# Layer norm behind the experts: offsets and one over the deviation brought by the transposing products

## The chip, the core and the metric

The kernel runs on one core of a Trainium2 chip. Its engines are TensorE (PE, with its weight load PEld), VectorE (DVE), ScalarE (ACT), GpSimd (POOL) and SyncE (SP); each takes its own instructions strictly in order and waits on semaphores for the others. The metric is the device time of one execution in microseconds (us), lower is better.

## What is computed

Two blocks of two layers each on 256 tokens of width 1024. The change sits at the end of both layers of the first block, in the layer norm behind the mixture of experts:

```python
for l in range(DEPTH):                    # two layers
    mix = hybrid_mixer(h, ...)            # attention
    x = layer_norm(ALPHA * x + mix, ln1_g[l], ln1_b[l])
    ffn = grouped_moe(x, ...)             # 16 experts, 2 of them for each token
    x = layer_norm(ALPHA * x + ffn, ln2_g[l], ln2_b[l])   # here
```

with y = (x - mean) * rsqrt(var + eps) * g + b along the 1024 columns of a token. Behind the first layer comes the second layer's mixer, behind the second layer the first mixer of the second block (a gated linear recurrence).

## The kernel before

The 256 tokens stand as two blocks of 128 rows (b = 0, 1), the 1024 columns as two halves (q = 0, 1). Every matrix product of a weight with the tokens wants the tokens transposed, and split into a high part (`xh`, rounded by ACT) and a low part (`xl`, the rest, subtracted by DVE); products are then high by high, low by high and high by low. Weights are split in the same way.

In `moe` the experts go in eight pairs. `down` (products `pdn`) gives a pair's rows, split into `oh` and `ol`; `spread` adds them to the token rows in four PSUM banks `py[b][q]`, eight products a pair. While the last pair is under way, `pre()` prepares the next part's first weights: `ready` rounds them on ACT (line 215) and subtracts on DVE, or on POOL for the units named by `pool` (line 217). This is `mixer_first` (products `pk` follow, in `mixer`) behind the first layer and `hgrn_first` (products `pv`, in `hgrn`) behind the second.

Then 16 filler products (`warm`, line 224) are queued on PE, and `layer_norm` runs. For each block: two statistics and their merge on DVE, the square root on ACT, and for each half two DVE steps (line 393): (y - mean) * g, and times one over the deviation plus b. The result `xn` is turned by four PE transposes (line 228) into a bank `pt`, which ACT reads as `xh` (line 363) and DVE subtracts to `xl` (line 364). DVE's steps follow each other in the order written, through `issue_after`; where no such tie is given, a scheduler puts the instructions of each engine in order when the program is built. The fields `s.after` tie the first five weight splits of the next part (line 166, 167) behind the norm.

A `pb` bank is one of four PSUM banks, a `pa` bank one of four others.

Of the kernel before, what the change touches and what calls it, by code (L numbers as in the profile page):

```python
# [10 lines left out]
F32 = mybir.dt.float32  # L11
F32R = mybir.dt.float32r
# [3 lines left out]
AF = mybir.ActivationFunctionType  # L16
ALU = mybir.AluOpType
# [3 lines left out]
T = 256  # L21
# [9 lines left out]
WM = 16  # L31
# [47 lines left out]
class Halves:  # L79


    def __init__(s, tiles):
        s.t = tiles
# [13 lines left out]
class Net:  # L97
# [7 lines left out]
    def __init__(s, ctx, tc, A, dump=None):  # L105
        s.ctx, s.tc, s.nc, s.A, s.dump = ctx, tc, tc.nc, A, dump or {}
        e = ctx.enter_context
        s.cp = e(tc.tile_pool(name="cp", bufs=1))
        s.ring = e(tc.tile_pool(name="ring", bufs=s.RING))
        s.weave, s.steps = None, 0  # L110
        s.after = []
        s.st = e(tc.tile_pool(name="st", bufs=1))
        s.dr = e(tc.tile_pool(name="dr", bufs=1, space=bass.MemoryType.DRAM))
        s.ps = e(tc.tile_pool(name="ps", bufs=4, space=bass.MemoryType.PSUM))
        s.consts()
# [44 lines left out]
    def split(s, h, l, src, g=None, pool=False):  # L160
        nc = s.nc
        with ExitStack() as es:
            for ins in s.after[:1] and s.after.pop(0):
                es.enter_context(s.tc.issue_after(ins))
            if g is None:
                nc.scalar.activation(h, src, AF.Copy)  # L166
                i = (nc.gpsimd if pool else nc.vector).tensor_tensor(l, src, h.bitcast(F32), op=ALU.subtract)  # L167
                s.low = i.ins
            else:
                nc.scalar.activation(h, src, AF.Copy, scale=g)  # L170
                nc.vector.scalar_tensor_tensor(l, src, g, h.bitcast(F32), op0=ALU.mult, op1=ALU.subtract)
# [33 lines left out]
    def ready(s, pieces, n=512, pool=()):  # L205

        s.units = []
        for k0 in range(0, 8, 2):
            if k0 % 4 == 0:
                H, L = (s.raw().bitcast(F32R)[:, :4 * n].rearrange("p (k n) -> p k n", k=4) for _ in range(2))  # L210
                s.units.append((k0, H, L))
            k = slice(k0 % 4, k0 % 4 + 2)
            for c0, src in pieces(k0):
                c = slice(c0, c0 + src.shape[2])
                s.nc.scalar.activation(H[:, k, c], src, AF.Copy)
                e = s.nc.gpsimd if k0 // 2 in pool else s.nc.vector
                e.tensor_tensor(L[:, k, c], src, H[:, k, c].bitcast(F32), op=ALU.subtract)

    def warm(s, n):

# [158 lines left out]
    def layer_norm(s, y, gb, out=None, added=False):  # L379


        nc, v = s.nc, s.nc.vector
        sl = [slice(q * 512, (q + 1) * 512) for q in range(2)]
        st = [s.st.tile([128, 2, 6], F32, tag="bst", name="bst", bufs=2) for _ in range(2)]
        mv = [s.st.tile([128, 4], F32, tag="mv", name="mv", bufs=2) for _ in range(2)]
        x = lambda b, q: s.xn[:, b, sl[q]]
        prev, low, act = [], {}, []

        def dve(f, *a, **k):
            with ExitStack() as es:  # L390
                for i in prev[-1:]:
                    es.enter_context(s.tc.issue_after(i))
                prev.append(f(*a, **k).ins)  # L393

        def moments(b, q):
            if not added:
                dve(v.scalar_tensor_tensor, x(b, q), x(b, q), ALPHA, y[b][q], op0=ALU.mult, op1=ALU.add)
            dve(v.bn_stats, st[b][:, q], y[b][q] if added else x(b, q))
            if q:
                dve(v.bn_aggr, mv[b][:, 0:2], st[b])  # L400
                act.append(nc.scalar.activation(mv[b][:, 2:3], mv[b][:, 1:2], AF.Sqrt, bias=s.eps[:, 0:1]).ins)

        def affine(b, q):
            dve(v.scalar_tensor_tensor, x(b, q), y[b][q] if added else x(b, q), mv[b][:, 0:1], gb[:, 0, sl[q]],
                op0=ALU.subtract, op1=ALU.mult)
            if not q:
                dve(v.reciprocal, mv[b][:, 3:4], mv[b][:, 2:3])
            dve(v.scalar_tensor_tensor, x(b, q), x(b, q), mv[b][:, 3:4], gb[:, 1, sl[q]], op0=ALU.mult, op1=ALU.add)
            if out is not None:
                nc.sync.dma_start(out[b * 128:(b + 1) * 128, sl[q]], x(b, q))  # L410
            else:
                a, low[b, q] = s.xT_high(s.xn[:, b], b, q)
                act.append(a.ins)

        def lows(*bq):
            for i in bq if out is None else ():
                dve(low[i])
        with s.tc.high_priority():
            for q in range(2):
                moments(0, q)  # L420
            for q in range(2):
                affine(0, q)
            for q in range(2):
                moments(1, q)
            lows((0, 0), (0, 1))
            for q in range(2):
                affine(1, q)
            lows((1, 0), (1, 1))
        s.after = [(act[-1], prev[-1])] * 5


    def rms(s, p, n, pool):
# [618 lines left out]
    def moe(s, li, y, pre):  # L1051
        nc, A = s.nc, s.A
        v = nc.vector
        with ExitStack() as es:
            mp = es.enter_context(s.pool("mo"))
# [14 lines left out]
            py = [[], []]  # L1070
# [15 lines left out]
            xTe, PT = {}, {}  # L1086

            def sources():

                for p in range(9):  # L1090
                    for n, w, k, m in (("g", A["w_gate"], 8, p), ("u", A["w_up"], 8, p), ("d", A["w_down"], 4, p - 1)):
                        if 0 <= m < 8:
                            o = "e (k p) f -> p e k f" if n == "d" else "e (p k) f -> p e k f"
                            wv = w[li, 2 * m:2 * m + 2].rearrange(o, p=128)
                            for k0 in range(0, k, k // 4):
                                yield wv[:, :, k0:k0 + k // 4]
            src = list(sources())
            place = list(islice(chain(s.FILL, cycle([c for c in s.FILL if c not in "mpx"])), len(src)))
            n0, loaded, todo = len(s.FILL), {}, iter(range(len(src)))
            m = s.FILL.index("m")  # L1100
# [3 lines left out]
            def load(i):  # L1104
                if i < len(src) and i not in loaded:
                    loaded[i] = s.chunks(src[i], place[i])
# [7 lines left out]
            def onehot(g):  # L1114

                es_ = slice(4 * g, 4 * g + 4)
                P = mp.tile([128, 2, 4, 64], F32R, tag="P", name="P")
                for b in range(2):
                    i = v.tensor_tensor(P[:, b], s.iota[:, None, :].to_broadcast([128, 4, 64]),
                                        rs[:, b, es_, None].to_broadcast([128, 4, 64]), op=ALU.is_equal).ins  # L1120
                return P, i
# [61 lines left out]
            def turn(ac):  # L1183
                pt = s.pb("pat")
                for c in range(4):
                    s.tr(pt[:, c * 128:(c + 1) * 128], ac[:, c * 128:(c + 1) * 128])
                v.tensor_copy(aT, pt.rearrange("p (c e s) -> p c e s", c=4, e=2))
# [22 lines left out]
            with s.tc.manual_schedule(engines={mybir.EngineType.PE}):  # L1210
                P, i = onehot(0)
                with s.tc.issue_after(i):
                    for c in (0, 4):
                        low_rows(v, 1, slice(c, c + 4))
                i = slots(0, P)
                for p in range(8):
                    ac = gate_up(p, None if p else lambda: gates(0, P))
                    if not p:
                        with s.tc.issue_after(i):
                            residual()  # L1220

                        for j in range(n0):
                            load(j)
                    if p:
                        os_[p - 1] = down()
                    turn(ac)
                    if p >= 2:
                        spread(p - 2, *os_.pop(p - 2))
                    if p % 2 and p < 7:
                        slots(p // 2 + 1, onehot(p // 2 + 1)[0])  # L1230
                    if p == 2:
                        s.overflow(li, ga, ov, rs, cnt, xnh, xnl, py)
                spread(6, *os_[6])
                o = down()
                gb = s.load_gb(s.places, A["ln2_g"][li], A["ln2_b"][li], "raw5")
                pre()
                s.xh, s.xl = s.new_xT()
                spread(7, *o)
            s.warm(WM)
            s.layer_norm(py, gb, added=True)  # L1240


    def hgrn_first(s):
# [355 lines left out]
```

## Time and profile before

| what | value |
|---|---|
| median of 3 runs | 1365.07 us |
| lowest and highest run | 1357.44 and 1366.09 us |
| profiled execution | 1362.14 us, of it 1360.4 us span on the engines |
| PE busy in the span | 1303.4 us (96%) |
| DVE, ACT, POOL busy | 769.6, 587.5, 79.0 us |
| first layer norm behind the experts | about 361 to 377 us in the span |
| second one | about 720 to 740 us in the span |

The profile is of one execution; its places are given in microseconds from the span's start. PE is the engine that is busy nearly all the time, so what counts is where PE waits, and how much work it is given.

### The profile page before, as it was taken

How to read it: one execution, taken by the hardware profiler on the slowest of the kernel's cores; microseconds unless marked ns; L12 is line 12 of the kernel's file. 1: busy time of each engine (PE TensorE's matmuls, PEld its weight loads, DVE VectorE, ACT ScalarE, POOL GpSimd, SP SyncE). 2: the span in 40 equal slices, each digit the busy share in tenths (PEclk: the TensorE clock that was granted, in tenths of full speed). 3: DMA queues.
4: the chain of work that ended last, by engine and by line, in shares of the span. 5: the costliest groups of instructions: out<-in, count | busy, mean ns of one | idle time of the engine just before them, and what ended most of it. 6: DMA issues, size and time to landing. Idle time of an engine off the chain costs nothing.

```text
span 1360.4 us, 20419 instructions
## 1 busy us (share of the span) xinstructions
PE 1303.4 (96%) x7933; PEld 950.2 (70%) x7933; DVE 769.6 (57%) x1611; ACT 587.5 (43%) x1107; POOL 79.0 (6%) x94
## 2 busy tenths in 40 slices
PE   7899999999989999999998999999999999999997
PEld 6787543443488663443445988889998787899986
DVE  4775520110468562111116678879885677888855
ACT  5585410110266841110104424456665376566642
POOL 3000100000200010000002143000000000000000
PEclk8899999999999999999999999999999999999999
DMA  9585799999984478999999730565553465565500
GB/s 300 194 310 182 259 410 407 409 409 408 351 302 155 157 267 334 409 408 409 409 408 330 249 124 1 186 216 191 187 212 125 133 210 184 181 224 186 206 12 31
DMA packets 153639, 343.03 MB, mean 252 GB/s; under 512 B 13377, under 2 KB 84999, under 8 KB 153536
## 3 DMA queue, kind: packets, MB, share of 16 engines
q1 hardware_dynamic: 149408, 330.14, 66.4%
q0 software_dynamic: 3808, 11.24, 2.4%
q8 instruction: 66, 1.08, 0.3%
q10 hardware_dynamic: 320, 0.26, 0.1%
q14 instruction: 37, 0.30, 0.1%
HBM read 340.53 MB, written 1.07 MB: 251 GB/s over the span
## 4 chain that ended last, share of the span: by engine, by line
PE 51%; DVE 3%; ACT 1%; issue 1%; DMA 1%; POOL 0%; ACTq 0%; DVEq 0%
PE pb L174 19%; PE y L174 12%; PE pv L174 3%; PE pdn L174 3%; PE pgg L174 3%; PE pgu L174 3%; PE pl L174 2%; PE ptk L174 2%; DVE xn L393 1%; PE py L174 1%; PE pkv L174 1%; PE po L174 1%; PE pt L228 1%; DVE wl L167 1%; DMA raw<-in_hgrn_w_in 1%
## 5 line engine op out<-in xcount | busy, mean ns | idle before, releaser
L167 DVE TENSOR_TENSOR wl<-raw,wh 128x1024 fp32r<-128x1024 f32 (+1 forms) x208 | 248.3, 1200 | 86.2 <-ACT wh L166 84.3
L166 ACT ACTIVATE wh<-raw 128x1024 fp32r<-128x1024 f32 (+1 forms) x208 | 213.7, 1035 | 70.2 <-PE y L174 62.1
L174 PE MATMUL pb<-xh,wl 128*128 128x256 f32 (+1 forms) x944 | 132.5, 281 | 1.6 <-DVE wl L167 1.6
L174 PE MATMUL pb<-xh,wh 128*128 128x256 f32 (+1 forms) x944 | 133.5, 281 | 0.5 <-ACT wh L166 0.5
L174 PE MATMUL pb<-xl,wh 128*128 128x256 f32 (+1 forms) x944 | 132.4, 280 | 0.0
L1180 DVE SCALAR_TENSOR_TENSOR misc<-misc,gs,pgu 128x512 f32<-128x512 f32 x16 | 12.0, 748 | 208.6 <-PE pgu L174 145.3
L174 PEld LDWEIGHTS pb<-xh,wh 128*128 128x128 f32 (+1 forms) x944 | 120.3, 187 | 2.1 <-ACT wh L166 0.7
L174 PEld LDWEIGHTS pb<-xh,wl 128*128 128x128 f32 (+1 forms) x944 | 119.9, 187 | 2.2 <-DVE wl L167 2.0
L174 PEld LDWEIGHTS pb<-xl,wh 128*128 128x128 f32 (+1 forms) x944 | 119.9, 187 | 0.1
L174 PE MATMUL pgg<-raw,xTe 128*64 128x512 f32 x480 | 108.1, 602 | 5.2 <-PEq L1011 5.2
L174 PE MATMUL pgu<-raw,xTe 128*64 128x512 f32 x512 | 112.7, 592 | 0.0
L174 PE MATMUL pdn<-raw,misc 128*64 128x512 f32 x496 | 109.3, 592 | 0.0
L166 ACT ACTIVATE xh<-pdn 128x512 fp32r<-128x512 f32 x32 | 19.1, 597 | 195.6 <-PE pdn L174 195.6
L174 PEld LDWEIGHTS pgu<-raw,xTe 128*64 128x64 f32 x512 | 37.2, 137 | 71.3 <-issue 65.7
L174 PEld LDWEIGHTS pdn<-raw,misc 128*64 128x64 f32 x496 | 36.1, 137 | 69.7 <-issue 68.0
L174 PEld LDWEIGHTS pgg<-raw,xTe 128*64 128x64 f32 x480 | 34.3, 138 | 69.4 <-issue 60.7
L167 DVE TENSOR_TENSOR xl<-pdn,xh 128x512 fp32r<-128x512 f32 x32 | 22.0, 687 | 100.4 <-ACT xh L166 94.4
L1179 ACT ACTIVATE misc<-pgg 128x512 f32<-128x512 f32 x16 | 9.6, 597 | 138.8 <-PE pgg L174 138.8
L174 PE MATMUL y<-wl,gh 128*128 128x512 f32 x176 | 68.7, 390 | 0.0
L174 PE MATMUL y<-wh,gl 128*128 128x512 f32 x176 | 68.6, 390 | 0.0
L174 PE MATMUL y<-wh,gh 128*128 128x512 f32 x176 | 68.2, 389 | 0.0
L174 PE MATMUL y<-wl,xh 128*128 128x512 f32 x128 | 51.6, 404 | 0.0
(381 smaller groups left out, 2238.6 us busy)
## 6 DMA issues: line engine op xcount, KB each, us to landing
raw<-in_w_up SPq DMA_DIRECT2D x128, 512.0 KB, 10.2
raw<-in_w_down SPq DMA_DIRECT2D x124, 512.0 KB, 10.2
raw<-in_w_gate SPq DMA_DIRECT2D x120, 512.0 KB, 10.2
raw<-in_ffn_w_in SPq DMA_DIRECT2D x44, 1024.0 KB, 5.6
raw<-in_ffn_w_out SPq DMA_DIRECT2D x22, 1024.0 KB, 4.9
raw<-in_hgrn_w_in SPq DMA_DIRECT2D x16, 1024.0 KB, 9.4
raw<-in_w_o SPq DMA_DIRECT2D x8, 1024.0 KB, 11.4
raw<-in_w_in SPq DMA_DIRECT2D x6, 1024.0 KB, 7.5
```

What stands on the lines that cost most here:

```text
L166: nc.scalar.activation(h, src, AF.Copy)
L167: i = (nc.gpsimd if pool else nc.vector).tensor_tensor(l, src, h.bitcast(F32), op=ALU.subtract)
L174: s.last = s.nc.tensor.matmul(out, lhsT, rhs, start=start, stop=stop, skip_group_check=True).ins
L228: return s.nc.tensor.transpose(out, in_, s.ident[:k, :k])
L393: prev.append(f(*a, **k).ins)
L1179: nc.scalar.activation(sg, ps[0], AF.Silu)
L1180: v.scalar_tensor_tensor(ac, sg, gs[:, p:p + 1], ps[1], op0=ALU.mult, op1=ALU.mult)
```

## The change

A new function `sum_norm` takes the place of `layer_norm` in `moe`. DVE makes only (y - mean) * g. ACT writes `dg`, the identity with row t scaled by one over the deviation of token t. The turned tile is now a sum of two products in PSUM: the offsets (b's columns by the identity, `offsets`) and xn by `dg` (`turned`). `xn` itself gets its factor and offset in four DVE steps at the end. Further, `s.behind` ties the rounding of the next part's first weights behind the last pair's own rounding, and the DVE subtractions of those weights are held (`s.held`) and issued inside `sum_norm`, half of them between the blocks' statistics and half behind the first block's low parts.

```diff
@@ in split
-                nc.scalar.activation(h, src, AF.Copy)
+                s.high = nc.scalar.activation(h, src, AF.Copy).ins
@@ in ready
-                s.nc.scalar.activation(H[:, k, c], src, AF.Copy)
-                e = s.nc.gpsimd if k0 // 2 in pool else s.nc.vector
-                e.tensor_tensor(L[:, k, c], src, H[:, k, c].bitcast(F32), op=ALU.subtract)
+                with ExitStack() as es:
+                    if s.behind:
+                        es.enter_context(s.tc.issue_after(s.behind))
+                    s.nc.scalar.activation(H[:, k, c], src, AF.Copy)
+                low = (src, H[:, k, c].bitcast(F32), L[:, k, c])
+                if s.behind and k0 // 2 not in pool:
+                    s.held.append(low)
+                else:
+                    e = s.nc.gpsimd if k0 // 2 in pool else s.nc.vector
+                    e.tensor_tensor(low[2], low[0], low[1], op=ALU.subtract)
@@ new
+    def sum_norm(s, y, gb, dg):
...
+        def seq(f, *a, **k):
+            e = id(f.__self__)
+            with ExitStack() as es:
+                if e in last:
+                    es.enter_context(s.tc.issue_after(last[e]))
+                last[e] = f(*a, **k).ins
+        act = nc.scalar.activation
+
+        def moments(b):
+            for q in range(2):
+                seq(v.bn_stats, st[b][:, q], y[b][q])
+            seq(v.bn_aggr, mv[b][:, 0:2], st[b])
+            seq(act, mv[b][:, 2:3], mv[b][:, 1:2], AF.Sqrt, bias=s.eps[:, 0:1])
+
+        def centred(b, q):
+            seq(v.scalar_tensor_tensor, x(b, q), y[b][q], mv[b][:, 0:1], gb[:, 0, sl[q]], op0=ALU.subtract,
+                op1=ALU.mult)
+            if not q:
+                seq(v.reciprocal, mv[b][:, 3:4], mv[b][:, 2:3])
+                seq(act, dg[:, b], s.ident, AF.Copy, scale=mv[b][:, 3:4])
+
+        def offsets(q):
+            p = s.pb("pt")
+
+            for j in range(4):
+                c = 4 * q + j
+                s.mm(p[:, j * 128:(j + 1) * 128], gb[:, 1, c * 128:(c + 1) * 128], s.ident, not j, False)
+            return p
+
+        def turned(b, q, p):
+            for j in range(4):
+                c = slice((4 * q + j) * 128, (4 * q + j + 1) * 128)
+                s.mm(p[:, j * 128:(j + 1) * 128], s.xn[:, b, c], dg[:, b], False, True)
+            pv = p.rearrange("p (a t) -> p a t", a=4)
+            h, l = (m.t[q][:, :, b * 128:(b + 1) * 128] for m in (s.xh, s.xl))
+            seq(act, h, pv, AF.Copy)
+            low[b, q] = lambda: seq(v.tensor_tensor, l, pv, h.bitcast(F32), op=ALU.subtract)
...
+        n = len(s.held) // 2
+        with s.tc.high_priority():
+            ps = [offsets(q) for q in range(2)]
+            moments(0)
+        s.warm(WM)
+        with s.tc.high_priority():
+            for q in range(2):
+                centred(0, q)
+                turned(0, q, ps[q])
+            held(n)
+            moments(1)
+            for q in range(2):
+                low[0, q]()
+            held(n)
+            for q in range(2):
+                centred(1, q)
+                turned(1, q, offsets(q))
+            for q in range(2):
+                low[1, q]()
+        s.after = [(last[id(nc.scalar)], last[id(v)])] * 5
+        for b in range(2):
+            for q in range(2):
+                seq(v.scalar_tensor_tensor, x(b, q), x(b, q), mv[b][:, 3:4], gb[:, 1, sl[q]], op0=ALU.mult, op1=ALU.add)
@@ in moe
+                s.behind = s.high
                 pre()
+                s.behind = None
...
-            s.warm(WM)
-            s.layer_norm(py, gb, added=True)
+            dg = mp.tile([128, 2, T], F32R, tag="PT", name="dg", bufs=2).bitcast(F32)[:, :, :128]
+            s.sum_norm(py, gb, dg)
```

The change alters the order that the scheduler builds. The rows below are instructions as they stand in an engine's queue, with the line of the code, the operation, what it writes and reads, and its size; "x16" is so many in a row.

PE, at the end of the first layer's experts, before: the last pair's `down`, then its `spread` into the four banks.

```order
L174 MATMUL pdn<-raw,misc 64x512 x16
L174 MATMUL py<-xh,PT 128x512
L174 MATMUL py<-xl,PT 128x512
L174 MATMUL py<-xh,PT 128x512
L174 MATMUL py<-xl,PT 128x512
```

The same place now; `pt<-c,gb` is four products of offsets for a half (c holds the identity), `warm` is a filler.

```order
L175 MATMUL pdn<-raw,misc 64x512 x3
L175 MATMUL pt<-c,gb 128x128 x8
L175 MATMUL pdn<-raw,misc 64x512 x13
L175 MATMUL py<-xh,PT 128x512
L175 MATMUL py<-xl,PT 128x512
L175 MATMUL py<-xh,PT 128x512
L232 LDWEIGHTS negI
L232 MATMUL warm<-mgtb,negI 128x512
L232 LDWEIGHTS negI
L232 MATMUL warm<-mgtb,negI 128x512
L175 MATMUL pt<-c,gb 128x128 x4
L175 MATMUL py<-xl,PT 128x512
```

Eight offset products moved into the `down` products, and two fillers and four offset products ahead of the second half's low product. The second layer's end reads alike. Behind `spread` stand 13 fillers (14 in the second layer), then eight products `pt<-dg,xn`.

ACT, in the second layer's mixer behind the norm, before: the turned halves of block 1, the query and key norm's sums (`rmsj`, `rms`, `rmsn`: three steps for each block of `pk`) and the splits of the next weights (`wh`).

```order
L363 ACTIVATE xh<-pt 128x4x128 x2
L436 ACTIVATE rmsj,rms<-pk 128x256
L437 ACTIVATE rms<-rms,eps 128x1
L680 ACTIVATE rmsn<-pk,rms 128x256
L166 ACTIVATE wh<-raw 128x1024 x2
L166 ACTIVATE wh<-raw 128x8x64
L166 ACTIVATE wh<-raw 128x8x32
L166 ACTIVATE wh<-raw 128x768
L436 ACTIVATE rmsj,rms<-pk 128x256
```

The same place now.

```order
L455 ACTIVATE xh<-pt 128x4x128 x2
L521 ACTIVATE rmsj,rms<-pk 128x256
L522 ACTIVATE rms<-rms,eps 128x1
L765 ACTIVATE rmsn<-pk,rms 128x256
L521 ACTIVATE rmsj,rms<-pk 128x256
L522 ACTIVATE rms<-rms,eps 128x1
L765 ACTIVATE rmsn<-pk,rms 128x256
L167 ACTIVATE wh<-raw 128x1024 x2
```

The three steps of block 1 moved ahead of all the splits; PE's products `pb` behind `pk` need the first `wh`.

ACT, behind the second layer's norm, before: `V` is the copy of a finished block of `pv`, `lb` a small table for which another function table is loaded.

```order
L363 ACTIVATE xh<-pt 128x4x128
L1365 ACT_TABLE_LOAD
L1365 ACTIVATE lb<-lb 128x16
L166 ACTIVATE wh<-raw 128x1024
L1357 ACTIVATE V<-pv 128x512
L166 ACTIVATE wh<-raw 128x1024 x3
```

The same place now.

```order
L1445 ACTIVATE V<-pv 128x512
L1453 ACT_TABLE_LOAD
L1453 ACTIVATE lb<-lb 128x16
L1445 ACTIVATE V<-pv 128x512
L167 ACTIVATE wh<-raw 128x1024 x4
```

The copy of block 1 moved ahead of the first split, which the next `pv` products need.

## Rows read from the trace of the kernel before

**Rows 1.** Stretches: us, busy us (count) of PE, PEld, DVE, ACT, POOL, clock, DMA, GB/s

```profile
350.00:361.50 11.50, 11.50 (x55) 5.55 (x53) 2.09 (x4) 1.41 (x4) 0.00 (x0) 1.00 0.89 280
...
720.70:729.80 9.10, 6.77 (x31) 3.21 (x29) 8.82 (x11) 5.68 (x8) 4.73 (x2) 1.00 1.07 355
```

**Rows 2.** Timeline of the first norm: start, us, engine, line, operation [idle before <- released by]

```profile
354.46 7.09 PE L174 MATMUL pdn<-raw,misc 128*64 128x512 f32 x32
...
360.76 0.60 ACT L166 ACTIVATE xh<-pdn 128x512 fp32r<-128x512 f32 x1 [9.91 <-PE pdn L174]
...
364.02 0.50 PE L174 MATMUL py<-xl,PT 128*128 128x512 f32 x1 [1.10 <-DVE xl L167]
...
364.55 0.70 DVE L393 BATCH_NORM_STATS2 bst<-py 128x6 f32<-128x512 f32 x1 [0.59 <-PE py L174]
...
365.28 2.98 PE L224 MATMUL warm<-mgtb,negI 128*128 128x512 bf16 x13
...
368.10 0.60 PE L228 MATMUL pt<-c,xn 128*128 128x128 f32 x4
...
369.44 0.45 PE L174 MATMUL pk<-raw,xh 128*128 128x392 f32 x1
```

**Rows 3.** The single products of offsets' kind: timeline of PE at 398 us

```profile
398.21 5.40 PE L174 MATMUL px<-ikT,iqT 128*128 128x128 f32 x32
```

**Rows 4.** Timeline of the second norm

```profile
719.96 0.60 ACT L166 ACTIVATE xh<-pdn 128x512 fp32r<-128x512 f32 x1 [9.91 <-PE pdn L174]
...
722.17 0.50 PE L174 MATMUL py<-xl,PT 128*128 128x512 f32 x1
...
723.45 3.41 PE L224 MATMUL warm<-mgtb,negI 128*128 128x512 bf16 x15
...
725.07 5.49 POOL L217 TENSOR_TENSOR raw<-raw 128x1024 fp32r<-128x1024 f32 x2 [27.99 <-ACT raw L215]
...
725.68 2.65 DVE L393 SCALAR_TENSOR_TENSOR xn<-xn,mv,gb 128x512 f32<-128x512 f32 x1
...
729.79 0.50 PE L174 MATMUL pv<-raw,xh 128*128 128x512 f32 x1 [0.53 <-ACT xh L363]
```

**Rows 5.** Line 393's steps, by form: count, min/median/max ns, first and last start

```profile
L393 DVE SCALAR_TENSOR_TENSOR xn<-xn,mv,gb x40: 741/752/2651, 366.7 to 1356.5; 128x512 f32<-128x512 f32 x40
```

**Rows 6.** Timeline behind the first norm, in the second layer's mixer

```profile
376.87 0.38 ACT L436 ACTIVATE rmsj<-pk 128x256 f32<-128x256 f32 x1
...
378.28 3.56 ACT L166 ACTIVATE wh<-raw 128x1024 fp32r<-128x1024 f32 x5
378.32 1.59 PE L174 MATMUL pk<-raw,xh 128*128 128x392 f32 x8
...
380.46 1.46 PE L174 MATMUL pb<-xh,wh 128*128 128x256 f32 x11
...
382.64 1.21 PE L174 MATMUL pb<-xh,wl 128*128 128x256 f32 x8 [0.71 <-DVE wl L167]
```

**Rows 7.** Timeline behind the second norm

```profile
744.16 1.09 PE L174 MATMUL pv<-wh,xh 128*128 128x512 f32 x4
744.36 0.60 ACT L1357 ACTIVATE V<-pv 128x512 f32<-128x512 f32 x1 [1.95 <-PE pv L174]
744.85 2.94 ACT L166 ACTIVATE wh<-raw 128x1024 fp32r<-128x1024 f32 x3
...
747.22 0.73 PE L174 MATMUL pv<-wl,xh 128*128 128x512 f32 x2 [0.29 <-DVE wl L167]
```

**Rows 8.** The chain that ended last, behind the second norm: start, us, what

```profile
747.22 8.90 PE pv L174 x37
```

**Rows 9.** Timeline of PE after a wait in the experts, first and second layer

```profile
224.66 7.09 PE L174 MATMUL pgg<-raw,xTe 128*64 128x512 f32 x32 [2.78 <-PEq L1011]
...
582.17 8.76 PE L174 MATMUL pgg<-raw,xTe 128*64 128x512 f32 x32 [2.44 <-PEq L1011]
```

**Rows 10.** The stretch of the second of these waits, columns as in rows 1

```profile
580.00:584.00 4.00, 1.82 (x6) 0.69 (x8) 0.00 (x0) 0.00 (x0) 0.00 (x0) 0.77 1.02 402
```

More of the change, by code (lines that the diff above doesn't have):

```diff
@@ L111, in __init__ @@
         s.after = []
+        s.behind, s.held = None, []
         s.st = e(tc.tile_pool(name="st", bufs=1))
@@ L429, in layer_norm, with held @@
         s.after = [(act[-1], prev[-1])] * 5
+    def sum_norm(s, y, gb, dg):
+        nc, v = s.nc, s.nc.vector
+        sl = [slice(q * 512, (q + 1) * 512) for q in range(2)]
+        st = [s.st.tile([128, 2, 6], F32, tag="bst", name="bst", bufs=2) for _ in range(2)]
+        mv = [s.st.tile([128, 4], F32, tag="mv", name="mv", bufs=2) for _ in range(2)]
+        x = lambda b, q: s.xn[:, b, sl[q]]
+        last, low = {}, {}
+        def seq(f, *a, **k):
[30 more added lines that the diff above has]
+            low[b, q] = lambda: seq(v.tensor_tensor, l, pv, h.bitcast(F32), op=ALU.subtract)
+        def held(n):
+            for _ in range(n):
+                src, h, l = s.held.pop(0)
+                seq(v.tensor_tensor, l, src, h, op=ALU.subtract)
+        n = len(s.held) // 2
[21 more added lines that the diff above has]
+                seq(v.scalar_tensor_tensor, x(b, q), x(b, q), mv[b][:, 3:4], gb[:, 1, sl[q]], op0=ALU.mult, op1=ALU.add)
```

## The prediction

> **What bounds the kernel now.** I read the page first: PE is busy for 96% of the span, and the chain that ended last is mostly PE. So a change counts by the waits that it takes from PE, and by the work that it adds there. Then the stretches around the two norms [rows 1]. In the last `down` and what stands ahead of it PE has no gap at all: 11.50 us busy in 11.50. In the second norm it is busy for 6.77 of 9.10, and 3.41 of that is filler [rows 4]; about 5.7 us there are not work. Last the timelines, where the reader is to follow one thread: ACT rounds the last pair's rows, PE spreads them, DVE takes statistics, filler runs, PE turns the tile, ACT copies it, PE begins `pk` or `pv`. In the first norm that is 360.76, 364.02, 364.55, 365.28, 368.10 and 369.44 [rows 2].
>
> **The change, part by part.** The order of each queue is fixed when the program is built, so I follow the new order with the old durations.
>
> *Offsets in the `down` products.* A single product in full precision shows on PE as two records. The 32 records from 398.21 are eight products of 128 and eight of 256 columns, 48 units of 128 in 5.40 us: 0.11 a record, 0.225 a product of 128 [rows 3]. Eight offset products cost 1.8, and they stand where PE has no gap [rows 1], so all of it is on the path, once in each norm. The gap that might hide them would be a wait for weights there, and there is none in 354.46 to 361.5 [rows 2].
>
> *Last pair first.* In the first norm the second half's low product came 3.26 after the first rounding (360.76 to 364.02) [rows 2], since a weight's rounding and subtraction stood between. In the second it came 2.21 after (719.96 to 722.17) [rows 4]: the pair's parts stood first there already, and the new order moves nothing. Gain 1.05 in the first norm, 0 in the second.
>
> *Two fillers and four offsets ahead of that low product.* The four cost 0.9; a filler is 0.23 (2.98 for 13) [rows 2], and most of the two lies in PE's wait for DVE. I take 1.05, between 0.9 and 1.36. The last `py` product is later by 1.8 - 1.05 + 1.05 = 1.8 in the first norm, by 1.8 + 1.05 = 2.85 in the second.
>
> *Filler.* 13 of them now stand ahead of the first turning product. In the first norm they begin at 365.28 + 1.8 = 367.1 and end at 370.1. DVE's thread to the old transposes took 3.55 (364.55 to 368.10), and one step of 0.75 [rows 5] has left it, so its data is there some 0.5 or more before; the filler, which was cover, decides. Eight products (1.8) and one filler follow, so `pk` begins at 372.1 against 369.44: +2.65. In the second norm filler begins at 723.45 + 2.85 = 726.3, 14 take 3.2, then one offset, eight products and three offsets, 2.7: `pv` begins at 732.2 against 729.79, +2.4.
>
> The old second norm had a loss that goes: DVE's second step took 2.65 us [rows 4] where its median is 0.75 [rows 5], beside POOL's subtractions from 725.07 on. That step leaves the thread, which is why the second norm isn't worse by its 2.85; the new filler takes the rest. The held subtraction of DVE now stands beside POOL's second one. It may be stretched by nothing or by those 1.9; it delays block 1's statistics and so its `dg`, for which PE then waits. I take 1.0, the middle, in the second norm, and 0 in the first, where POOL's tiles are half as wide or less.
>
> The Trainium skill (SBUF — State Buffer, Who interferes with whom) says that a DVE instruction with both inputs in SBUF and a GpSimd instruction that reads SBUF share a port pair, and that the later one waits for all of the other. The row of 2.65 agrees. By the rule alone the held subtraction would wait as that step did, and the sum would be 0.9 more; without it, 1.0 less.
>
> *Turning block 1.* A `pk` product takes 0.18 (eight from 378.32 and four more until 380.46) [rows 6], 48 of them 8.55. Four offsets (0.9) and eight turning products (1.8) now lie among them: 372.1 + 11.25 = 383.35 against 380.46, +2.9. In the second norm a `pv` product takes 0.24 (8.90 for 37) [rows 8], 48 of them 11.55, with 1.8 of turning and the wait of 1.0: 746.55 against 744.16 [rows 7], +2.4.
>
> *ACT's order behind.* PE's next products `pb` need the first split `wh`. Before, ACT had begun it at 378.28, while PE was still at `pk` [rows 6]. Now the sums of block 1 stand ahead of it, and they need the end of `pk`. From a block's sums to the first split is 1.41 (376.87 to 378.28) [rows 6], the split itself 0.98 (2.94 for three) [rows 7], and a little to PE: 2.5 in which PE has nothing. `pb` begins 2.9 + 2.5 = 5.4 late. Of the old wait of 0.71 for the low split [rows 6] about 0.45 goes, since that split has time now: +4.95. The four deferred steps on `xn` stand ahead of block 0's small steps on DVE, 3 us long; they are over before `pk` ends and cost nothing by themselves. Behind the second norm block 1's `V` now stands ahead of the first split: it begins 0.2 after the last `pv` product and takes 0.5 (744.36 to 744.85) [rows 7], then 0.98 and 0.1: 1.8. With 0.3 of an old wait gone [rows 7], 2.4 + 1.8 - 0.3 = +3.9.
>
> Sum: 4.95 + 3.9 = 8.9 us. Behind both places the order is as before, and PE is nearly full there, so I let nothing be won back. Against the profiled execution's 1362.14 that is 1371.0. This execution lies 2.9 below the median of the runs shown (1365.07), which would give 1374.0; the runs spread from 1357.44 to 1366.09. I forecast 1372. From both sides: without ACT's waits and without `dg`'s 3.6 is left; with the stretches in full 10.
>
> **Rivals.** *The shorter thread decides (faster).* If PE's added products fall into its waits and filler, what is left is the gain: 1.05 of last pair first, 0.75 of the step that left the thread in each norm, and 1.9 of POOL's stretch: 4.45, so 1357.7. For it speaks that 5.7 us of the second norm are no work [rows 1, 4]. It decides as soon as the offsets in `down` find a gap and ACT reaches its splits before PE wants them. Against it: 11.50 of 11.50 [rows 1], and two queues whose order is plain.
>
> *The clock falls (slower by more).* The new waits of PE are 2.5 and 1.8. In the experts a wait of 2.78 left the next run of products at 7.09, a wait of 2.44 made the same run 8.76 [rows 9], and there the granted clock reads 0.77 [rows 10], so the clock went to the lower of its levels, 1.2 GHz, for a part of it. One such fall costs 1.7, one at each place 3.4: 1374 to 1376, on the median's side 1377.
>
> *It doesn't do what it says.* Last pair first does nothing in the second norm; that is in the sum already. Were it void in the first too, 1 more: 1373.
>
> **How the numbers follow.** The forecast with its small variants gets 0.62, 1366 to 1376. The clock gets 0.2, since one of two such waits fell. The shorter thread gets 0.18; its 1357.7 lies outside the range but part of its spread inside. A measurement of this kernel can tell about 1% from no change, here 13.65 us, above 1378.7 or below 1351.4. The forecast and the faster rival lie within that, and only the clock with underrated waits goes beyond: faster 0.02, within 0.88, slower 0.10. Range 1361 to 1380.
>
> **What the changed profile would show.** In the last `down`: eight products `pt<-c,gb` as one run of about 1.8 with no idle before it; idle there would favour the faster rival. In the second norm no step on `xn` from `py` above 0.8. Turning products that begin as the filler ends, ACT's copy long idle before: right; filler already over, and PE idle for `dg`: my thread of DVE is too short. A wait of PE for `wh` (ACT) of about 2.5 ahead of the first `pb` behind `pk`, and of about 1.8 ahead of `pv<-wh`: right; under 0.5: wrong by 4. A granted clock under 0.9 within a few us behind either: the second rival.
>
> What would make all of it wrong: a gain or loss far from the two norms, where the order is the same and I counted nothing, or a run of PE there that takes up the delay because its weights, not its inputs, come last.

## The result, and the profile after

The changed kernel takes 1377.42 us (median of 7 runs, 1371.15 to 1378.66), the kernel before in the same session 1362.44 (7 runs, 1357.44 to 1366.09). The ratio is 1.0101, 95% interval 1.0076 to 1.0125. The profiled execution of after took 1378.62, its span is 1376.6 against 1360.4.

The timeline of PE in the first norm, kernel after (start, us, engine, line, operation, idle before and who ended it):

```profile
356.51 1.93 PE L175 MATMUL pdn<-raw,misc 128*64 128x512 f32 x6
358.38 2.05 PE L175 MATMUL pt<-c,gb 128*128 128x128 f32 x16
360.36 6.22 PE L175 MATMUL pdn<-raw,misc 128*64 128x512 f32 x26
366.51 0.50 PE L175 MATMUL py<-xh,PT 128*128 128x512 f32 x1
...
370.22 2.98 PE L232 MATMUL warm<-mgtb,negI 128*128 128x512 bf16 x13
373.04 1.95 PE L175 MATMUL pt<-dg,xn 128*128 128x128 f32 x16
...
374.85 0.53 PE L175 MATMUL pk<-raw,xh 128*128 128x392 f32 x1
...
379.38 2.05 PE L175 MATMUL pt<-dg,xn 128*128 128x128 f32 x16 [0.29 <-ACT dg L455]
...
386.25 0.88 PE L175 MATMUL pk<-raw,xl 128*128 128x392 f32 x4
390.32 1.22 PE L175 MATMUL pb<-xh,wh 128*128 128x256 f32 x8 [3.19 <-ACT wh L167]
```

The first `py` product of the kernel before, on the same timeline:

```profile
361.48 0.49 PE L174 MATMUL py<-xh,PT 128*128 128x512 f32 x1
```

The reader is to see four things against it and [rows 2, 6]. From the first `down` product to the first `py` product it is 366.51 - 356.51 = 10.00, before 361.48 - 354.46 = 7.02. The turning products begin as the filler ends, with no idle time. Block 1's turning products wait 0.29 for `dg`. And ahead of `pb` PE has nothing for 3.19, where before it went straight on.

DVE, ACT and POOL (GpSimd) in the first norm and at that wait, kernel after, timelines of the three engines:

```profile
371.19 0.73 DVE L455 SCALAR_TENSOR_TENSOR xn<-py,mv,gb 128x512 f32<-128x512 f32 x1
371.84 2.76 DVE L455 TENSOR_TENSOR raw<-raw 128x512 fp32r<-128x512 f32 x2
...
377.12 1.03 DVE L455 TENSOR_TENSOR raw<-raw 128x512 fp32r<-128x512 f32 x2
...
382.70 2.73 DVE L455 SCALAR_TENSOR_TENSOR xn<-xn,mv,gb 128x512 f32<-128x512 f32 x4
...
387.17 0.17 DVE L683 TENSOR_SCALAR iw<-pk 128x8 f32<-128x8 f32 x1 [0.18 <-PE pk L175]
...
387.56 0.17 DVE L535 TENSOR_TENSOR ropet<-pk,c 128x16 f32<-128x16 f32 x1
```

```profile
371.31 0.40 ACT L455 ACTIVATE dg<-c,mv 128x128 f32<-128x128 f32 x1
...
387.82 0.38 ACT L521 ACTIVATE rmsj<-pk 128x256 f32<-128x256 f32 x1 [0.33 <-DVE ropet L535]
...
389.22 3.55 ACT L167 ACTIVATE wh<-raw 128x1024 fp32r<-128x1024 f32 x5
```

```profile
371.35 3.88 POOL L225 TENSOR_TENSOR raw<-raw 128x512 fp32r<-128x512 f32 x3 [2.14 <-ACT raw L219]
```

ACT's sums of a block stand ahead of the splits, as foretold, but they don't begin when `pk` ends. They wait for DVE's small steps on the same tile of `pk`. For block 0 these steps stand behind the four deferred steps on `xn`, but that sets nothing here: ACT is done with block 0's sums and idle for 0.33 before block 1's begin at 387.82. PE's 3.19 are 0.69 from the end of `pk` to these sums, 1.40 for them and 1.10 from the first split to `pb`. The held subtractions on weights (`raw<-raw`) show one more thing: the first two took 2.76 with GpSimd's subtractions beside them, the last two 1.03 without.

The second norm, kernel after, timelines of PE, of DVE and of POOL:

```profile
724.75 1.93 PE L175 MATMUL pdn<-raw,misc 128*64 128x512 f32 x6
...
734.74 0.50 PE L175 MATMUL py<-xh,PT 128*128 128x512 f32 x1
...
738.45 3.19 PE L232 MATMUL warm<-mgtb,negI 128*128 128x512 bf16 x14
...
744.40 3.66 PE L175 MATMUL pv<-raw,xh 128*128 128x512 f32 x15
747.90 1.95 PE L175 MATMUL pt<-dg,xn 128*128 128x128 f32 x16
...
758.97 1.19 PE L175 MATMUL pv<-wh,xh 128*128 128x512 f32 x4 [1.63 <-ACT wh L167]
```

```profile
740.07 1.22 DVE L455 TENSOR_TENSOR raw<-raw 128x1024 fp32r<-128x1024 f32 x1
```

```profile
737.48 2.38 POOL L225 TENSOR_TENSOR raw<-raw 128x1024 fp32r<-128x1024 f32 x1 [29.31 <-ACT raw L219]
740.06 3.43 POOL L225 TENSOR_TENSOR raw<-raw 128x1024 fp32r<-128x1024 f32 x1 [0.20 <-ACT raw L219]
```

Against [rows 4, 7]: no step on `xn` is stretched any more, PE doesn't wait for the second `dg` at all, and PE waits 1.63 for `wh`. The two stretches behind PE's waits, kernel after, busy time of PE, PEld, DVE, ACT and POOL, then the mean granted clock (1.00 is TensorE's full 2.4 GHz), DMA share and GB/s:

```profile
390.32:396.32 6.00, 5.96 (x35) 5.75 (x36) 4.37 (x6) 3.57 (x6) 0.00 (x0) 0.72 1.07 374
...
758.97:764.97 6.00, 5.93 (x18) 4.44 (x19) 4.61 (x4) 2.79 (x3) 0.00 (x0) 0.72 1.10 348
```

Both are below full clock: for a part of each the clock was at its lower level, 1.2 GHz. The prediction named this as the second rival.

The delay of after against before, read from the starts of the same products in the two timelines, lies where it was looked for and is larger. After is 2.05 late when the first norm begins; about 1.6 of that is at one wait in the experts of the first layer, the one of 2.78 [rows 9], behind which the clock fell in this execution and not in that of before. It lies ahead of all that the change touches. The first norm and what follows add 8.8 (4.95 foretold), 0.3 comes on the way to the second, which adds 5.1 (3.9 foretold), and nothing is added behind. Sum 16.2, the difference of the spans. In the table each norm is counted from its own first `down` product.

| against before, us | foretold | measured |
|---|---|---|
| first norm: `down` | +1.8 | +2.97 |
| start of `pk` | +2.65 | +3.35 |
| end of `pk` | +2.9 | +4.5 |
| first `pb` | +5.4 | +7.8 |
| less wait for the low split | -0.45 | -0.92 |
| clock behind it | 0 (rival: 1.7) | +1.9 |
| second norm: `down` | +1.8 | +2.97 |
| start of `pv` | +2.4 | +3.5 |
| end of these `pv` products | +2.4 | +1.9 |
| first `pv<-wh` | +4.2 | +3.7 |
| end, with the clock | +3.9 | +5.1 |

### The profile page after: what moved, and what is told of

Read it like the earlier page. It is cut to its first block, busy times and chain, and to the rows that moved or that the text cites. A ratio compares the mean times of both kernels' runs of the same rounds, so it can differ in the third digit from the quotient of the medians.

```text
span 1376.6 us, 20607 instructions
## 1 busy us (share of the span) xinstructions
PE 1320.7 (96%) x8029; PEld 966.1 (70%) x8029; DVE 767.9 (56%) x1611; ACT 589.5 (43%) x1111; POOL 79.1 (6%) x94
## 3 DMA queue, kind: packets, MB, share of 16 engines
HBM read 340.53 MB, written 1.07 MB: 248 GB/s over the span
## 4 chain that ended last, share of the span: by engine, by line
PE 52%; DVE 3%; ACT 1%; issue 1%; POOL 0%; DVEq 0%; ACTq 0%
PE pb L175 19%; PE y L175 12%; PE pv L175 3%; PE pdn L175 3%; PE pgg L175 3%; PE pgu L175 2%; PE pl L175 2%; PE ptk L175 2%; PE py L175 1%; PE pkv L175 1%; PE po L175 1%; DVE wl L168 1%; PE pt L175 1%; DVE xn L401 1%; PE pt L236 1%
```

## Experiments

The theory after the result: the loss is made of places, not of the new arithmetic. Offsets stand where PE has no gap and break a pair of `down` products (1.0 more in each norm than their own length); ACT's sums and `V` stand ahead of the splits; the waits that come of it let the clock fall. Rivals: the offsets are dear in themselves, the tie of the last pair costs, or there is a loss elsewhere.

**e1_pairs: offsets behind four `down` products instead of three.**

```diff
-            ps = [offsets(q) for q in range(2)]
+            with s.tc.issue_after(s.dn[3]):   # s.dn: down's products in order
+                ps = [offsets(q) for q in range(2)]
```

> The changed kernel with the eight offsets of block 0 moved on by one `down` product, behind four of the sixteen instead of three. Theory (a broken pair): two `down` products of 64 columns each run side by side, a pair in 0.86; three ahead of the offsets leave one product alone on either side, so the stretch from the first `down` product to the first `py` product takes 10.0 (16 products were 7.02 before) although the offsets are 2.0 of it. Behind four it should take 9.0 in both norms, and the whole 2.0 less than the changed kernel. Rival (offsets are dear in themselves, or the change between their shape and that of `down` is): it stays at 10.0 and the time with it. The range of both: 9.0 or 10.0, ratio to before 1.0085 or 1.010.

Measured: ratio 1.0069 (1.0044 to 1.0094). PE's timeline in the first norm of this kernel:

```profile
356.91 1.94 PE L175 MATMUL pdn<-raw,misc 128*64 128x512 f32 x8
358.77 2.05 PE L175 MATMUL pt<-c,gb 128*128 128x128 f32 x16
360.75 5.37 PE L175 MATMUL pdn<-raw,misc 128*64 128x512 f32 x24
366.06 0.49 PE L175 MATMUL py<-xh,PT 128*128 128x512 f32 x1
```

Eight records take the 1.94 in which six took 1.93 in after, and 24 take 5.37 instead of 6.22 for 26. From the first `down` product to `py` it is 9.15 instead of 10.00. So a broken pair it is: 0.85 in each norm. The spans of the two profiles differ by 1.8 (1374.8 against 1376.6), about as much. The ratio moved by more, some 4, but the intervals overlap. The clock of the two profiles doesn't explain it, with a mean of 0.988 in both. Here it fell behind the first wait alone and stayed down for longer (0.51 over the next 6 us, against 0.72 behind each wait in after).

**e2_order: ACT's old order behind both norms.**

```diff
+    if b and s.highs:                     # sums of block 1, first norm
+        es.enter_context(s.tc.issue_after(s.highs[4]))
     r = s.rms(pk[b][:, 0:256], 256, mp)
...
+    if first and b:                       # V of block 1, second norm
+        splits(c0 + 512)
+        es.enter_context(s.tc.issue_after(s.highs[0]))
     evac(b, p)
```

> The changed kernel with ACT's old order behind the norms: the five splits `wh` ahead of block 1's sums in the first norm, two splits ahead of block 1's `V` in the second; nothing else moves. Theory (ACT's order makes PE wait, and the wait lets the clock fall): the wait of PE for `wh` goes from 3.2 to about 1.4 in the first norm (block 0's sums still stand ahead, and wait for DVE's steps on the same tile, which stand behind the deferred steps on xn), from 1.63 to 0 in the second, and the two stretches of 3.41 at granted clock 0.5 just behind go as well: 1.8 + 1.6 + 2 x 1.7 = 6 to 7 less than the changed kernel, ratio to before about 1.005. Rival (something else, a load of weights, holds the splits): the waits stay within 0.5 of 3.2 and 1.6. Second rival (the falls of the clock have nothing to do with these waits): the waits go, the falls at the same places stay, 3.4 less.

Measured: ratio 1.0052 (1.0035 to 1.0069), as expected. PE in this kernel behind each norm, and the stretch of the first:

```profile
388.11 1.21 PE L178 MATMUL pb<-xh,wh 128*128 128x256 f32 x8 [1.34 <-ACT wh L168]
...
754.14 1.09 PE L178 MATMUL pv<-wh,xh 128*128 128x512 f32 x4
```

```profile
388.11:394.11 6.00, 5.95 (x48) 5.75 (x49) 4.45 (x7) 4.60 (x10) 0.00 (x0) 1.00 1.09 360
```

The wait of 3.19 is 1.34, that of 1.63 is gone, and the clock is full behind both. What is left of the first wait is block 0's sums, which still stand ahead of the splits. The order of ACT, and the clock with it, makes about half of the loss.

**e3_nofirst: the new norm without the tie of the last pair.**

```diff
-                s.behind = s.high
```

> The changed kernel without the tie that puts the last pair's rounding ahead of the next weights' (ACT rounds weights and DVE subtracts where the queue put them before); the new norm stays. Theory (the loss is the new norm's: offsets in `down`, filler, ACT's order): the loss stays, within 2 us of the changed kernel, and about 1 more in the first norm, where the second half's low product comes later again. Rival (holding back the weights' rounding and subtraction is what costs, through the wait for the second `dg` and the late lows): most of the loss goes, 6 or more less than the changed kernel.

Without the tie the DVE subtractions of these weights aren't held either, so both go together. Measured: ratio 1.0078 (1.006 to 1.0096), 3 less than after with overlapping intervals. In the trace, counted from the start of the norm, the low `py` product is 1.1 later than in after, `pk` begins 1.3 later (four offsets of block 1 now stand ahead of it) and `pb` 0.3 earlier; the waits for `wh` are 3.19 and 1.63 again. Neither the tie nor the holding is the cause.

**e4_first: the kernel before with the tie alone.**

```diff
+                    if s.behind:
+                        es.enter_context(s.tc.issue_after(s.behind))
                     s.nc.scalar.activation(H[:, k, c], src, AF.Copy)
```

> The kernel before with the last pair's rounding ahead of the next weights' and nothing else of the change. Theory: the second half's low product in the first norm comes 2.2 behind the first rounding instead of 3.26, the transposes about 1 earlier or hidden by filler; second norm as before; the whole 0 to 1 less than before, ratio 0.999 to 1.000. Rival (the tie delays the next weights and so `pk`): the first `pk` waits for `raw`, 1 to 3 more than before.

Measured: ratio 1.0003 (0.9991 to 1.0014). PE's timeline of this kernel:

```profile
365.32 0.50 PE L175 MATMUL py<-xl,PT 128*128 128x512 f32 x1
...
366.60 3.63 PE L228 MATMUL warm<-mgtb,negI 128*128 128x512 bf16 x16
370.06 0.60 PE L232 MATMUL pt<-c,xn 128*128 128x128 f32 x4
371.41 0.63 PE L175 MATMUL pk<-raw,xh 128*128 128x392 f32 x2 [0.75 <-ACT xh L367]
```

The low product does come 1.05 earlier, counted against the start of the norm. But all 16 fillers now stand ahead of the transposes, where 13 stood, and `pk` waits 0.75 for ACT's copy that the other three had covered. `pb` comes 0.4 later than before. What last pair first gives, filler takes.

**e5_fill: twelve offsets in filler's place, 4 fillers.**

```diff
-            ps = [offsets(q) for q in range(2)]
+            with s.tc.issue_after(s.last):      # the last py product
+                ps = [offsets(q) for q in range(2)]
+                ps1 = offsets(0)
             moments(0)
-        s.warm(WM)
+        s.warm(4)
...
-                turned(1, q, offsets(q))
+                turned(1, q, offsets(q) if q else ps1)
```

> The changed kernel with twelve of the sixteen offset products of each norm moved to the place of the filler, behind the last `py` product, and filler cut from 16 products to 4. Theory (the place is what costs: in `down` and ahead of the low `py` product the offsets lie on the path, in filler's place they replace work that is none): the `down` stretch is 7.0 again (3.0 less), the two fillers and four offsets ahead of the low `py` product are gone (about 0.9 less), twelve offsets take the 2.9 of the filler; `pk` and `pv` start 3.9 earlier, the whole 6 to 8 less than the changed kernel, ratio to before 1.004 to 1.006. PE's wait for `wh` of 3.2 and 1.6 stays. Rival (DVE's thread to the turning products decides, not PE's work): PE waits for `dg` or xn by as much, and less than 4 is won.

Measured: ratio 1.0017 (0.9997 to 1.0037), its ten runs from 1360.89 to 1372.25. In the profiled execution (span 1370.1) `pb` is 3.95 earlier than in after, counted from the start of the norm, and the second norm ends 3.5 earlier, which is the theory's size; the waits for `wh` are still 3.19 and 1.63, with the clock lower behind both. The median gained more than the profile, and no trace shows why. The profiled execution is the second slowest of the ten, with a mean granted clock of 0.987; the five quickest had 0.990 to 0.994, which points to the clock without showing where.

**e6_free: as e2_order, with block 0's sums behind the splits too.**

```diff
-    if b and s.highs:
+    if s.highs:
```

> As e2_order, and the sums of block 0 stand behind the five splits too. Theory (what is left of the wait there, 1.34, is block 0's sums, which wait for DVE's steps on the same tile behind four deferred steps on xn): the wait of PE for `wh` at the first `pb` goes to 0, 1.0 to 1.4 less than e2_order, ratio to before about 1.004. Rival (the splits' weights arrive late, or the splits themselves are late for another reason): the wait stays above 1.

Measured: ratio 1.0043 (1.0026 to 1.0059). PE in this kernel:

```profile
387.62 1.11 PE L178 MATMUL pb<-xh,wh 128*128 128x256 f32 x8
389.79 1.21 PE L178 MATMUL pb<-xh,wl 128*128 128x256 f32 x8 [1.07 <-DVE wl L171]
```

DVE in this kernel, the first of block 1's small steps:

```profile
387.82 0.17 DVE L687 TENSOR_SCALAR iw<-pk 128x8 f32<-128x8 f32 x1 [1.05 <-PE pk L178]
```

The wait for ACT is gone, but PE now waits 1.07 for DVE's low split. That stands behind block 1's small steps, which begin when `pk` ends: DVE is idle for 1.05 ahead of them, so the deferred steps on `xn` have no part in it. The kernel before has this wait too, 0.71 behind three more products [rows 6]. From the end of `pk` to the products `pb<-xl,wh` 0.6 of the 1.34 is won. The theory's place was right; DVE's queue was the next to be late.

**e7_few: 12 fillers instead of 16 in the changed kernel.**

```diff
-        s.warm(WM)
+        s.warm(12)
```

> The changed kernel with 12 filler products in place of 16. Theory (filler decides when the turning products of block 0 begin; dg and xn had been ready for some 1.1): they begin 0.9 earlier in both norms, PE doesn't wait for DVE, the whole 1.5 to 2 less than the changed kernel. Rival (DVE's thread decides): no change, PE idle by 0.9 ahead of them. Third case (filler keeps the clock up): the granted clock falls in or behind the norms where it didn't, 1.7 more for each.

Measured: ratio 1.0091 (1.0074 to 1.0108), 1.4 less than after. PE in this kernel:

```profile
368.28 2.33 PE L232 MATMUL warm<-mgtb,negI 128*128 128x512 bf16 x10
370.67 0.71 PE L175 MATMUL pt<-c,gb 128*128 128x128 f32 x4
371.22 1.95 PE L175 MATMUL pt<-dg,xn 128*128 128x128 f32 x16
...
388.05 2.08 PE L175 MATMUL pb<-xh,wh 128*128 128x256 f32 x8 [3.56 <-ACT wh L167]
```

It moved differently than expected: two offsets of block 1 took the place of the missing filler, so the turning products begin 2.94 after the filler does, as in after (2.82). `pk` then ends 0.7 earlier, since these offsets no longer lie in it, and the wait for `wh` is 0.37 longer: with `pk` over earlier, block 0's sums, behind the deferred steps, now hold up block 1's. The experiment doesn't decide what sets the turning products; in e8_all and e9_none they begin right behind offsets that stand in filler's place, without idle time of PE.

**e8_all: e5_fill and e6_free together.**

```diff
+            with s.tc.issue_after(s.last):
+                ps = [offsets(q) for q in range(2)]
+                ps1 = offsets(0)
...
+        s.warm(4)
...
+    if s.highs:
+        es.enter_context(s.tc.issue_after(s.highs[4]))
```

> e5_fill and e6_free together: offsets in filler's place, all five splits ahead of the sums. Theory (the new norm loses by place and order alone, save for the turning products, which are dearer than transposes, and four offsets of block 1): down 7.0, no wait for `wh`, no fall of the clock behind the norms; what is left against the kernel before is about 1 for the turning products of block 0, less what DVE's shorter thread gives, and 1 to 2 for block 1, in each norm: ratio to before 0.999 to 1.003. Rival (there is a loss not yet seen, downstream or in contention): it stays above 1.004.

Measured: ratio 0.9989 (0.9977 to 1.0000), a hair below the expected range. PE in this kernel behind each norm:

```profile
382.51 1.10 PE L178 MATMUL pb<-xh,wh 128*128 128x256 f32 x8
...
744.77 1.09 PE L178 MATMUL pv<-wh,xh 128*128 128x512 f32 x4
```

No wait for `wh`, no lower clock behind the norms, `down` 7.02; the wait for the low split is as in e6_free. In the profile the first norm costs 0.5 up to the first `pb` against before, the second gives back about 2. No sign of another loss is left.

**e9_none: e8_all without the last filler.**

```diff
-        s.warm(4)
```

> As e8_all, without the last four filler products. Theory (filler decides, PE has other work for every wait there): four products of 0.23 go from each norm and nothing takes their place, 1.2 to 1.8 less than e8_all, ratio to before 0.997 to 0.998. Rival (they cover ACT's copy ahead of `pk` in the first norm and DVE's steps in the second): PE idle by as much, ratio 0.999 as e8_all. Third case: the clock falls behind the norms, 1.7 more each.

Measured: ratio 0.9984 (0.9966 to 1.0002). PE in the stretches of the two norms of this kernel:

```profile
363.00:370.00 7.00, 7.00 (x58) 6.83 (x56) 6.53 (x12) 5.02 (x13) 4.27 (x4) 1.00 1.08 368
721.00:730.00 9.00, 9.00 (x65) 8.18 (x64) 7.63 (x13) 5.36 (x9) 6.32 (x3) 1.00 1.07 352
```

PE is busy all the time with offsets and products, no filler, and the clock stays full. The ratio is just above what was expected, and its interval reaches 1, so this run by itself doesn't show it faster than before.

**e10_before_few: the kernel before with 12 fillers.**

```diff
-            s.warm(WM)
+            s.warm(12)
             s.layer_norm(py, gb, added=True)
```

> The kernel before with 12 filler products in place of 16 and nothing of the change, to see whether what e8_all and e9_none win is only filler. Theory (it isn't: in the kernel before, DVE's longer thread decides when the transposes begin, so filler there covers idle time): ratio 0.9995 to 1.0005; PE idle ahead of the transposes or of `pk` by what the filler took. Rival (filler decides there too): 0.9 less in each norm, ratio 0.9985.

Measured: ratio 1.0023 (1.0007 to 1.0039), slower; the expectation was too kind. PE in the second norm of this kernel, and the stretch behind:

```profile
727.23 2.76 PE L224 MATMUL warm<-mgtb,negI 128*128 128x512 bf16 x12
732.16 0.65 PE L228 MATMUL pt<-c,xn 128*128 128x128 f32 x4 [2.17 <-DVE xn L393]
```

```profile
733.00:739.00 6.00, 4.77 (x13) 3.58 (x14) 6.00 (x8) 2.35 (x4) 2.91 (x4) 0.50 1.03 346
```

PE waits 2.17 for DVE's stretched steps and the clock goes to its lower level for all of the next 6 us. In this profile the first norm takes as long as before, the second 1.9 longer. It is the slowest of the twelve executions. So in the old norm filler can't simply go, and what e8_all and e9_none save isn't filler alone.

**e11_second: the new norm of e9_none in the second place alone, the old one in the first.**

```diff
+            if li:
                 s.sum_norm(py, gb, dg)
+            else:
+                s.warm(WM)
+                s.layer_norm(py, gb, added=True)
```

> The new norm in the second place alone, with its offsets in filler's place, no filler and the splits ahead of `V` as in e9_none; the first norm is the old one word for word. Theory (the new norm wins where GpSimd's subtractions had stretched DVE's steps of the old one to 2.65 and 2.08, and wins nothing in the first): from the last `down` to the first `pv<-wh` some 2.5 to 3 less than before, nothing elsewhere, ratio to before 0.9975 to 0.9985. Rival (the two norms win alike): 1.2 less, 0.999.

Measured: 1360.34 against 1362.69, ratio 0.9980 (0.9971 to 0.9989): faster than both kernels. PE in the second norm of this kernel:

```profile
715.75 7.09 PE L178 MATMUL pdn<-raw,misc 128*64 128x512 f32 x32
...
725.53 3.73 PE L178 MATMUL pt<-c,gb 128*128 128x128 f32 x32
...
730.91 3.97 PE L178 MATMUL pv<-raw,xh 128*128 128x512 f32 x16
```

All sixteen offsets stand in filler's place and `pv` begins 730.91 - 715.75 = 15.16 after `down`, where it took 729.79 - 713.66 = 16.13 before. The stretch from `down` to the first `pv<-wh` (744.22) is 28.47 against 30.50, 2.0 less where 2.5 to 3 were expected; 0.6 more is won right behind, where PE had waited for the low split [rows 7]. No run separates what GpSimd's stretch, DVE's shorter thread and ACT's order have in it.

## Why the prediction was right, and where its sum fell short

The side and the places were right, 1377.42 lies in the range, and the loss was put where it arose: `down`, filler, ACT's sums and `V`, nothing elsewhere. The size was not: 8.9 foretold, 13.9 in the traces at the two norms, and 15.0 between the medians. So there is some luck in it: 1377.42 lies above the 1366 to 1376 that the forecast itself was given, where the second rival stood (up to 1377), and it got there by falls of the clock and by other terms that were too small.

*Offsets in the `down` products* (1.8 in each norm). This term is mis-sized: it measured 2.97. Their own length is 1.98 (358.38 to 360.36), near the 1.8. The other 1.0 is a pair that I didn't see: the `down` products run two by two, 16 products in 7.02 [rows 2], and three stand ahead of the offsets. e1_pairs shows 0.85 of it.

*Last pair first* (-1.05) against *two fillers and four offsets* (+1.05). The first came true as a start time and paid nothing on its own (e4_first). Together they measured -0.1 in the first norm, where 0 was foretold, and 0.9 in the second, where the fillers and offsets alone stood in the sum with 1.05.

*Filler decides* held in after: it ended as the turning products began, and `dg` and `xn` had been ready since 371.7 and 371.9, against 373.04. In e8_all and e11_second offsets do the filler's duty.

*Turning block 1* (+0.25 from the start to the end of `pk`) measured 1.1: `pk` products took 0.19 each, not 0.18, with 0.29 of waiting. The wait for the second `dg` in the second norm, taken at 1.0, measured 0: the held subtraction took 1.22, and GpSimd's, which started with it, took 3.43, where the one before had taken 2.38. By the Trainium skill (SBUF — State Buffer, Who interferes with whom) the one that comes later waits for all of the other; the trace agrees in that only one of the two was stretched. Which came later it doesn't show, since they start 0.01 apart. I had reckoned with the wrong one, and with the wrong norm: in the first I took 0, and there DVE's held subtractions took 2.76 beside GpSimd's instead of 1.03, which made the second `dg` late and PE wait 0.29.

*ACT's order behind* (2.5 and 1.8) was the right mechanism, as e2_order shows, and too small in the first norm: PE's wait is 3.19, not 2.5. What the sum left out is that ACT's sums wait for DVE's small steps on the same tile of `pk`: 0.69 from the end of `pk` to the sums of block 1. The rest is near, 1.40 for the 1.41 and 1.10 for the 0.98 and "a little". "The four deferred steps cost nothing by themselves" held in this kernel, where ACT waits between the two blocks' sums. In the second norm 1.63 measured against 1.8.

*The clock falls*, given 0.2, came about at both places, 1.9 and 1.4 (5.1 measured, less the 3.7 at `pv<-wh`; an old wait of 0.29 gone is in it). Taking the price from two waits of the experts [rows 9, 10] was sound; the chance was too low, for by those two a fall is as likely as not. The longer wait, 3.19, lies above both of them, the shorter, 1.63, below.

*The shorter thread decides* named its own condition, offsets that find a gap and splits ahead of PE's wish. e8_all makes that condition true and comes to 0.9989, e11_second to 0.9980. So the rival's mechanism exists; its condition was not met by the change as it stood.

## What to carry to other kernels

Products that are added to shorten another engine's thread belong where that thread makes PE wait, in filler's place, and not in a run without gaps; look there for products that go in pairs, since an odd place breaks one. After any change of a norm, compare the order of the next engine's queue behind it: here about half of the loss came from sums and a copy that moved ahead of splits. And when a wait goes, look for what is late next, as DVE's low split was in e6_free.

## What the runs showed of the hardware

Two `down` products of 64 columns run side by side: their four records take 0.86 (16 products, 32 records, in 7.02). A single one, cut off by another product, takes the same 0.86 (1.93 for six records, 1.94 for eight).

The clock and PE's waits: behind each wait of 3.19 or 3.56 (after, e1_pairs, e3_nofirst, e5_fill, e7_few) the mean granted clock of the next 6 us was between 0.51 and 0.74; behind the wait of 1.63 of the same five kernels it was 0.72 twice (after, e5_fill) and full three times; behind 1.34 in e2_order, and behind some 1.07 for the low split in e6_free and e8_all, it was full. So a wait of the same length can have either outcome. That this makes part of the spread between runs of one kernel isn't shown, as each was profiled once; it fits that the two quickest runs of after, 1371.15 and 1374.21, had mean granted clocks of 0.995 and 0.990 and the other five 0.987 or 0.988.

The clock also stays up without filler: in e9_none offsets stand in its place and the clock was full in both norms.

Where subtractions of DVE and of GpSimd ran at the same time, one side took longer: in the first norm two of DVE's took 2.76 instead of 1.03, in the second one of GpSimd's took 3.43 where the one before took 2.38.
